# An Lp-pool over 128 MB on one core: three input slots of 51.5 KB per partition in place of four of 32 KB, stores of two loads each, and four smaller loads at the end

## The chip, the cores and the metric

The kernel runs on one core of a Trainium2 chip. Its time is the device time of one execution in microseconds (us). Three of its engines matter here: ACT (ScalarE), DVE (VectorE) and SP (SyncE, which here only sends out transfers). The experiments ran in three sets, each set on one chip beside runs of the kernel before: the control, the quarter rows, the two large end loads and the early half store on one chip, the others on a second. All runs quoted were of the fast state, with a granted clock of 1.000. The profiled executions give a span, from the first to the last instruction; the timed number is about 2 us longer (span 393.7 us, time 395.79 us).

## The reference, cut to what matters

```python
def setup_inputs():
    batch, channels, length = 32, 256, 4096          # 134.2 MB of float32
    ...                                              # p = 2.0, kernel_size = 4

def reference(x, p, kernel_size):
    ...
        window = np.abs(x[:, :, start:end]) ** p
        result[:, :, i] = (np.mean(window, axis=-1)) ** (1.0 / p)
```

Windows do not overlap: four neighbours are squared, summed, divided by four, and the root is taken. So 134.22 MB are read and 33.55 MB written, once each, and any contiguous piece of the flat input whose length is a multiple of four gives a contiguous piece of the output. The kernel is free in how it cuts the data.

## The kernel before

Every load is 128 partitions by 8192 columns (32 KB a row), in four input slots. ACT squares in place, DVE adds groups of four, ACT takes the root in place. Four loads fill one output tile, which is stored at once. All loads go out from SP's queue, most stores from ACT's. The stores of the two groups before the last load are held until all loads have been issued, so that they cover the compute that is left after the last load lands.

```python
    W = 8192
    CH = 4096
    GROUP = 4
    LAST = 1
    ...
    in_pool = ctx.enter_context(tc.tile_pool(name="in_pool", bufs=4))
    out_pool = ctx.enter_context(tc.tile_pool(name="out_pool", bufs=2))
    ...
    def load(i):
        xt = in_pool.tile([P, W], fp32)
        nc.sync.dma_start(out=xt, in_=x_block(i))
    ...
        if i == first + g - 1 and c + CH == W and group_of[i] not in held:
            nc.scalar.dma_start(out=out_block(group_of[i]), in_=ot)
    ...
    for gi in sorted(held):
        nc.sync.dma_start(out=out_block(gi), in_=ots[gi])
```

Of the kernel before, what the change touches and what calls it, by code (L numbers as in the profile page):

```python
# [1 line left out]

# [4 lines left out]


@with_exitstack
def kernel(  # L10
    ctx: ExitStack,
    tc: tile.TileContext,
    x: bass.AP,
    p: float,
    kernel_size: int,
    out: bass.AP,
):








    nc = tc.nc

    assert float(p) == 2.0, "kernel specialized for p == 2"
    k = int(kernel_size)
    assert k == 4, "kernel specialized for kernel_size == 4"  # L30

    P = nc.NUM_PARTITIONS
    fp32 = mybir.dt.float32
    xf = x.rearrange("b c l -> (b c l)")
    of = out.rearrange("b c l -> (b c l)")
    total = xf.shape[0] // P

    W = 8192
    CH = 4096
    GROUP = 4  # L40
    LAST = 1
    n = total // W
    assert n * W == total


    groups = []
    i = 0
    while i < n - LAST:
        g = min(GROUP, n - LAST - i)
        groups.append((i, g))  # L50
        i += g
    groups += [(j, 1) for j in range(n - LAST, n)]
    held = {len(groups) - 1 - LAST - j for j in range(2)}
    group_of = {}
    for gi, (first, g) in enumerate(groups):
        for j in range(g):
            group_of[first + j] = gi

    in_pool = ctx.enter_context(tc.tile_pool(name="in_pool", bufs=4))
    out_pool = ctx.enter_context(tc.tile_pool(name="out_pool", bufs=2))  # L60
    last_pool = ctx.enter_context(tc.tile_pool(name="last_pool", bufs=1))
    ctx.enter_context(tc.manual_schedule())


    def x_block(i):
        first, g = groups[group_of[i]]
        block = xf[first * W * P:(first + g) * W * P].rearrange("(p w) -> p w", p=P)
        return block[:, (i - first) * W:(i - first + 1) * W]

    def out_block(gi):  # L70
        first, g = groups[gi]
        return of[first * W * P // k:(first + g) * W * P // k].rearrange("(p w) -> p w", p=P)

    xts = {}
    ots = {}

    def load(i):
        xt = in_pool.tile([P, W], fp32)
        nc.sync.dma_start(out=xt, in_=x_block(i))  # L79
        xts[i] = xt  # L80

    def root(i, c):
        first, g = groups[group_of[i]]
        ot = ots[group_of[i]]
        at = ((i - first) * W + c) // k
        o = ot[:, at:at + CH // k]
        nc.scalar.activation(  # L87
            out=o, in_=o, func=mybir.ActivationFunctionType.Sqrt, scale=1.0 / k,
        )
        if i == first + g - 1 and c + CH == W and group_of[i] not in held:  # L90
            nc.scalar.dma_start(out=out_block(group_of[i]), in_=ot)

    for i in range(3):
        load(i)

    pending = None
    for i in range(n):
        if i + 3 < n:
            load(i + 3)
        gi = group_of[i]  # L100
        first, g = groups[gi]
        if i == first:
            pool = last_pool if i >= n - LAST else out_pool
            ot = pool.tile([P, g * W // k], fp32)
            ots[gi] = ot
        for c in range(0, W, CH):
            xh = xts[i][:, c:c + CH]
            nc.scalar.activation(  # L108
                out=xh, in_=xh, func=mybir.ActivationFunctionType.Square,
            )  # L110
            at = ((i - first) * W + c) // k
            nc.vector.tensor_reduce(  # L112
                out=ots[gi][:, at:at + CH // k],
                in_=xh.rearrange("p (n j) -> p n j", j=k),
                axis=mybir.AxisListType.X, op=mybir.AluOpType.add,
            )
            if pending is not None:
                root(*pending)
            pending = (i, c)
    root(*pending)  # L120
    for gi in sorted(held):
        nc.sync.dma_start(out=out_block(gi), in_=ots[gi])


# [1 line left out]
_INS = ['x', 'p', 'kernel_size']  # L126
_OUTS = [((32, 256, 1024), 'float32')]

_NUMBERS = {'p': 2.0, 'kernel_size': 4}


# [26 lines left out]
```

## Time and profile before

| | before |
|---|---|
| time, median of the first 3 runs (of 6 with the comparison) | 395.79 us (395.73 us) |
| span | 393.7 us |
| DVE, ACT busy | 282.8 us, 294.7 us |
| bytes moved, mean rate over the span | 167.79 MB, 426 GB/s |
| data packets | 5248, and 656 of 4 B for semaphores (16 for each of the 41 transfers, which signal its end) |

The profile's page of the kernel before. The busy lines give tenths of busy time in 40 equal slices of the span; the DMA line is the mean of the 16 DMA engines, and the line below it what they moved. Then come the packets, the chain of work that ended last by engine, and the costliest groups of instructions (count, busy us, mean ns, idle before and what ended it):

```profile
span 393.7 us, 357 instructions
DVE 282.8 (72%) x64; ACT 294.7 (75%) x130; POOL 0.2 (0%) x4
DMA  8999998999999999999999999999999999999997
GB/s 350 446 430 426 426 426 373 449 446 430 433 426 426 426 430 453 440 430 433 426 426 426 426 449 443 427 433 430 426 426 426 443 446 433 430 433 426 426 435 314
DMA packets 5906, 167.79 MB, mean 426 GB/s; under 512 B 656, under 2 KB 656, under 8 KB 656
DMA 72%; ACT 17%; DVE 9%; SPq 0%; issue 0%; ACTq 0%
...
L112 DVE TENSOR_REDUCE ot<-xt 128x1024 f32<-128x4096 f32 x64 | 282.8, 4420 | 103.4 <-ACT xt L108 102.6
L108 ACT ACTIVATE xt<-xt 128x4096 f32<-128x4096 f32 x64 | 230.9, 3610 | 87.6 <-DMA xt<-in_x_dram 85.0
```

DMA is at nine tenths in every slice but the first, the seventh and the last, while ACT idles a quarter of the time, nearly all of it waiting for loads, and DVE as much, waiting for ACT. The chain is mostly landings of loads. The kernel is bound by the DMA engines, and only what keeps these from moving bytes can cost time.

The waits of SP, which issues the loads, and ACT's wait for the loads (us in total, times, longest us):

```profile
SPq L79 <- DVE ot L112: 293.7, 28, 12.5
SPq L79 <- DMA xt<-in_x_dram: 40.0, 7, 10.2
ACT xt L108 <- DMA xt<-in_x_dram: 85.0, 32, 10.9
```

SP's waits look enormous and cost nothing. SP waits for a slot to come free while the loads already issued are still being moved, as the DMA line shows.

The trace also records each DMA packet with its start, duration and size. In this kernel one row of a transfer is one packet, and for 95% of the time exactly 16 packets are under way, one for each engine. The kept records do not name the engine, so "per engine" below means summed over all packets and divided by 16. These numbers were worked out from those records:

```
size of the row    median duration on one engine
 8,192 B            309 ns
24,576 B            912 ns
32,768 B           1213 ns
first data packet starts at 1.75 us, the last ends at 392.48 us: 390.73 us between them
```

A straight line through these durations has 0.0368 ns per byte (27.2 GB/s on one engine, 435 GB/s on 16) and about 8 ns per packet. The Trainium skill, "DMA: Bandwidth & Descriptors", section "Where 436 GB/s comes from", puts the fabric's ceiling at 435 GB/s, and the slope agrees. The same section says that the HBM side binds at about 358 GB/s for HBM to SBUF; here the measured 426 GB/s decides otherwise. "HBM Reference", section "Specifications (TRN2)", has the reason: the 358 GB/s are a core's share when both cores of a pair stream, and a lone core gets about 425 GB/s, bounded by its DMA engines. No run here had both cores streaming.

### The profile page before, as it was taken

Reading aid. Unit: us, or ns where it says so; the run is one execution under the profiler, and the core shown is the slowest. Engines: PE = TensorE matmul, PEld = TensorE weight load, DVE = VectorE, ACT = ScalarE, POOL = GpSimd, SP = SyncE. Lnnn points to the kernel's source line nnn. Section 1 sums busy time; section 2 is a strip of 40 time slices with the busy share of each in tenths; the row PEclk is TensorE's granted clock in tenths of the full one; section 3 lists DMA queues with packets and bytes.
Section 4 is the critical chain, followed back from the end, with each engine's and each line's share of the span. In section 5 each row is a group of like instructions: output and inputs, shape, how many; then the busy total and the mean of one; then the engine's idle time right before and its main releaser. Section 6 shows DMA issues by size and latency. Waiting matters only on the chain.

```text
span 393.7 us, 357 instructions
## 1 busy us (share of the span) xinstructions
DVE 282.8 (72%) x64; ACT 294.7 (75%) x130; POOL 0.2 (0%) x4
## 2 busy tenths in 40 slices
DVE  0399996739976399764988559866598846999992
ACT  1699987469883798828988189863998819999981
POOL 0000000000000000000000000000000000000000
DMA  8999998999999999999999999999999999999997
GB/s 350 446 430 426 426 426 373 449 446 430 433 426 426 426 430 453 440 430 433 426 426 426 426 449 443 427 433 430 426 426 426 443 446 433 430 433 426 426 435 314
DMA packets 5906, 167.79 MB, mean 426 GB/s; under 512 B 656, under 2 KB 656, under 8 KB 656
## 3 DMA queue, kind: packets, MB, share of 16 engines
q1 hardware_dynamic: 4896, 141.56, 83.9%
q10 hardware_dynamic: 1008, 26.21, 15.5%
q14 instruction: 2, 0.02, 0.0%
HBM read 134.22 MB, written 33.55 MB: 426 GB/s over the span
## 4 chain that ended last, share of the span: by engine, by line
DMA 72%; ACT 17%; DVE 9%; SPq 0%; issue 0%; ACTq 0%
DMA xt<-in_x_dram 72%; ACT xt L108 14%; DVE ot L112 9%; ACT ot L87 2%; SPq L79 0%; ACTq L108 0%
## 5 line engine op out<-in xcount | busy, mean ns | idle before, releaser
L112 DVE TENSOR_REDUCE ot<-xt 128x1024 f32<-128x4096 f32 x64 | 282.8, 4420 | 103.4 <-ACT xt L108 102.6
L108 ACT ACTIVATE xt<-xt 128x4096 f32<-128x4096 f32 x64 | 230.9, 3610 | 87.6 <-DMA xt<-in_x_dram 85.0
L87 ACT ACTIVATE ot<-ot 128x1024 f32<-128x1024 f32 x64 | 67.0, 1047 | 4.2 <-DVE ot L112 3.4
L108 ACT ACT_TABLE_LOAD x1 | 1.3, 1283 | 0.7 <-PEq L139 0.7
L87 ACT ACT_TABLE_LOAD x1 | 1.3, 1283 | 0.0
L139 POOL MEMSET const-uint8-127<- 128x1 uint8 x1 | 0.1, 102 | 0.0
L139 POOL MEMSET const-bfloat16-1.0<- 128x1 bf16 x1 | 0.1, 101 | 0.0
L139 POOL MEMSET const-float32-0.0<- 128x1 f32 x1 | 0.1, 98 | 0.2 <-issue 0.2
L139 POOL MEMSET const-float32-1.0<- 128x1 f32 x1 | 0.1, 98 | 0.0
## 6 DMA issues: line engine op xcount, KB each, us to landing
xt<-in_x_dram SPq DMA_DIRECT2D x32, 4096.0 KB, 35.9
out_dram<-ot ACTq DMA_DIRECT2D x6, 4096.0 KB, 23.2
out_dram<-ot SPq DMA_DIRECT2D x1, 4096.0 KB, 34.1
out_dram<-ot SPq DMA_DIRECT2D x1, 3072.0 KB, 12.3
out_dram<-ot ACTq DMA_DIRECT2D x1, 1024.0 KB, 5.6
```

Of the source, the lines that this page charges most:

```text
L87: nc.scalar.activation(out=o, in_=o, func=mybir.ActivationFunctionType.Sqrt, scale=1.0 / k,)
L108: nc.scalar.activation(out=xh, in_=xh, func=mybir.ActivationFunctionType.Square,)
L112: nc.vector.tensor_reduce(out=ots[gi][:, at:at + CH // k], in_=xh.rearrange("p (n j) -> p n j", j=k), axis=mybir.AxisListType.X, op=mybir. ...
L139: nc = _bacc.Bacc("TRN2", target_bir_lowering=False, num_devices=1)
```

## The change

It uses the memory of a partition differently: three slots of 13,184 columns (51.5 KB) instead of four of 32 KB, and two output tiles of 25.8 KB. There are 18 large loads and four smaller ones, two to a slot, so that the compute left at the end comes in smaller pieces. Two loads make one store, and the last two outputs lie in input slots that are no longer needed. The stores of the last four groups all go out from SP's queue, after all loads. The arithmetic is the same.

```diff
-    W = 8192
-    CH = 4096
-    GROUP = 4
-    LAST = 1
+    W, O_W = 13184, 6592
+    X_SLOTS, O_SLOTS = 3, 2
+    slots = [[(W, [4416, 4384, 4384])]] * 18
+    slots += [[(6592, [3296, 3296])] * 2, [(6592, [3296, 3296]), (5056, [2528, 2528])]]
+    groups = [2] * 9 + [3, 1]
+    late = {7, 8, 9, 10}
+    in_x = {9, 10}
 ... (bookkeeping of loads, groups and columns)
-    in_pool = ctx.enter_context(tc.tile_pool(name="in_pool", bufs=4))
-    out_pool = ctx.enter_context(tc.tile_pool(name="out_pool", bufs=2))
-    last_pool = ctx.enter_context(tc.tile_pool(name="last_pool", bufs=1))
+    x_pool = ctx.enter_context(tc.tile_pool(name="x_pool", bufs=X_SLOTS))
+    o_pool = ctx.enter_context(tc.tile_pool(name="o_pool", bufs=O_SLOTS))
 ...
-    for i in range(3):
-        load(i)
+    while ahead < n and loads[ahead][0] < X_SLOTS - 1:
+        load(ahead)
+        ahead += 1
 ...
-    for gi in sorted(held):
-        nc.sync.dma_start(out=out_block(gi), in_=ots[gi])
+    for g in sorted(late):
+        store(g, nc.sync)
```

More of the change, by code (lines that the diff above doesn't have):

```diff
@@ L33 @@
     fp32 = mybir.dt.float32
+    Act = mybir.ActivationFunctionType
     xf = x.rearrange("b c l -> (b c l)")
@@ L36 @@
     total = xf.shape[0] // P
-    W = 8192
-    CH = 4096
-    GROUP = 4
-    LAST = 1
-    n = total // W
-    assert n * W == total
-    groups = []
-    i = 0
-    while i < n - LAST:
-        g = min(GROUP, n - LAST - i)
-        groups.append((i, g))
-        i += g
-    groups += [(j, 1) for j in range(n - LAST, n)]
-    held = {len(groups) - 1 - LAST - j for j in range(2)}
-    group_of = {}
-    for gi, (first, g) in enumerate(groups):
-        for j in range(g):
-            group_of[first + j] = gi
@@ L59 @@
-    in_pool = ctx.enter_context(tc.tile_pool(name="in_pool", bufs=4))
-    out_pool = ctx.enter_context(tc.tile_pool(name="out_pool", bufs=2))
-    last_pool = ctx.enter_context(tc.tile_pool(name="last_pool", bufs=1))
-    ctx.enter_context(tc.manual_schedule())
-    def x_block(i):
-        first, g = groups[group_of[i]]
-        block = xf[first * W * P:(first + g) * W * P].rearrange("(p w) -> p w", p=P)
-        return block[:, (i - first) * W:(i - first + 1) * W]
-    def out_block(gi):
-        first, g = groups[gi]
-        return of[first * W * P // k:(first + g) * W * P // k].rearrange("(p w) -> p w", p=P)
@@ L74 @@
-    xts = {}
-    ots = {}
-    def load(i):
-        xt = in_pool.tile([P, W], fp32)
-        nc.sync.dma_start(out=xt, in_=x_block(i))
-        xts[i] = xt
-    def root(i, c):
-        first, g = groups[group_of[i]]
-        ot = ots[group_of[i]]
-        at = ((i - first) * W + c) // k
-        o = ot[:, at:at + CH // k]
-        nc.scalar.activation(
-            out=o, in_=o, func=mybir.ActivationFunctionType.Sqrt, scale=1.0 / k,
-        )
-        if i == first + g - 1 and c + CH == W and group_of[i] not in held:
-            nc.scalar.dma_start(out=out_block(group_of[i]), in_=ot)
@@ L93 @@
-    for i in range(3):
-        load(i)
+    W, O_W = 13184, 6592
[5 more added lines that the diff above has]
+    in_x = {9, 10}
+    loads = [(s, sum(w for w, _ in slot[:j]), *slot[j]) for s, slot in enumerate(slots)
+             for j in range(len(slot))]
+    n = len(loads)
+    assert sum(w for _, _, w, _ in loads) == total
@@ new lines, with block @@
+    firsts = [sum(groups[:g]) for g in range(len(groups))]
+    assert sum(groups) == n
+    group_of = [g for g, count in enumerate(groups) for _ in range(count)]
+    columns = [sum(w for _, _, w, _ in loads[firsts[g]:firsts[g] + groups[g]])
+               for g in range(len(groups))]
+    x_pool = ctx.enter_context(tc.tile_pool(name="x_pool", bufs=X_SLOTS))
+    o_pool = ctx.enter_context(tc.tile_pool(name="o_pool", bufs=O_SLOTS))
+    ctx.enter_context(tc.manual_schedule())
+    def block(flat, g, div):
+        at, width = sum(columns[:g]) * P // div, columns[g] * P // div
+        return flat[at:at + width].rearrange("(p w) -> p w", p=P)
@@ new lines, with load, store, root @@
+    slot_tiles = {}
+    xs = {}
+    def load(i):
+        s, at, w, _ = loads[i]
+        if at == 0:
+            slot_tiles[s] = x_pool.tile([P, W], fp32, name="xt")
+        v = slot_tiles[s][:, at:at + w]
+        g = group_of[i]
+        src = sum(loads[j][2] for j in range(firsts[g], i))
+        nc.sync.dma_start(out=v, in_=block(xf, g, 1)[:, src:src + w])
+        xs[i] = v
+    ots = {}
+    def store(g, queue):
+        queue.dma_start(out=block(of, g, k), in_=ots[g])
+    def root(g, o, ends):
+        nc.scalar.activation(out=o, in_=o, func=Act.Sqrt, scale=1.0 / k)
+        if ends and g not in late:
+            store(g, nc.scalar)
@@ L96 @@
+    ahead = 0
+    while ahead < n and loads[ahead][0] < X_SLOTS - 1:
+        load(ahead)
+        ahead += 1
     pending = None
     for i in range(n):
-        if i + 3 < n:
-            load(i + 3)
-        gi = group_of[i]
-        first, g = groups[gi]
-        if i == first:
-            pool = last_pool if i >= n - LAST else out_pool
-            ot = pool.tile([P, g * W // k], fp32)
-            ots[gi] = ot
-        for c in range(0, W, CH):
-            xh = xts[i][:, c:c + CH]
-            nc.scalar.activation(
-                out=xh, in_=xh, func=mybir.ActivationFunctionType.Square,
-            )
-            at = ((i - first) * W + c) // k
+        s, _, w, chunks = loads[i]
+        while ahead < n and loads[ahead][0] < s + X_SLOTS:
+            load(ahead)
+            ahead += 1
+        g = group_of[i]
+        if i == firsts[g]:
+            pool, width = (o_pool, O_W) if g not in in_x else (x_pool, W)
+            t = pool.tile([P, width], fp32, name="ot" if g not in in_x else "xt")
+            ots[g] = t[:, 0:columns[g] // k]
+        at = sum(loads[j][2] for j in range(firsts[g], i)) // k
+        assert sum(chunks) == w
+        c = 0
+        for step in chunks:
+            v = xs[i][:, c:c + step]
+            nc.scalar.activation(out=v, in_=v, func=Act.Square)
+            o = ots[g][:, at + c // k:at + (c + step) // k]
@@ L112 @@
             nc.vector.tensor_reduce(
-                out=ots[gi][:, at:at + CH // k],
-                in_=xh.rearrange("p (n j) -> p n j", j=k),
+                out=o, in_=v.rearrange("p (n j) -> p n j", j=k),
                 axis=mybir.AxisListType.X, op=mybir.AluOpType.add,
@@ L118 @@
                 root(*pending)
-            pending = (i, c)
+            c += step
+            pending = (g, o, i == firsts[g] + groups[g] - 1 and c == w)
     root(*pending)
-    for gi in sorted(held):
-        nc.sync.dma_start(out=out_block(gi), in_=ots[gi])
+    for g in sorted(late):
+        store(g, nc.sync)
 _INS = ['x', 'p', 'kernel_size']
```

## The prediction

> **What bounds the kernel now.** The 16 DMA engines. The page gives 167.79 MB at a mean of 426 GB/s over a span of 393.7 us; the slices show DMA at 9 tenths nearly throughout, while DVE is busy 72% and ACT 75%. The chain of waits that ended last is 72% DMA landing of xt. In the trace's DMA packet records the first data packet starts at 1.8 us and the last ends at 392.5 us; packets follow one another on each engine without gaps. One row is one packet: 32,768 B takes 1213 ns, 24,576 B 912 ns, 8,192 B 309 ns. So a byte costs 0.0368 ns on one engine (27.2 GB/s, 435 GB/s for 16) and a packet about 8 ns more. The Trainium skill, "DMA: Bandwidth & Descriptors", section "Where 436 GB/s comes from", gives 435 GB/s as the fabric's ceiling, which this trace meets; its lower 358 GB/s for one core's HBM share does not bind here.
>
> Beyond that sum (388.6 us per engine) the 390.7 us between first and last packet hold only about 2.1 us: 0.6 us of slow first packets, 1.05 us where all 16 engines' packets took 2.2 us at once (58 us, just after the first store was issued), and about 0.4 us at the end and scattered.
>
> **What the change does.** Bytes are the same. Data packets fall from 5248 to 4224 (22 loads instead of 32, 11 stores instead of 9; 128 each), 64 fewer per engine at about 8 ns: 0.5 us. By size, estimated from the fit: 52,736 B 1947 ns, 26,368 B 978 ns; per engine the sum is 388.0 us against 388.6. Semaphore packets (9 ns each) give under 0.1 us.
>
> Compute moves but is not on the critical path: squares of 4384 columns about 3.85 us, reductions 4.73 us, roots 1.11 us; per load ACT 15.0 us and DVE 14.2 us against 15.6 us of transfer (19.5 with its share of stores). A slot comes free about 18.5 us after landing, when the other two slots still hold about 12 us of queued transfer, so three slots should not starve the queue. The old kernel's waits of loads on DVE (294 us in the waits of the SP queue) cost nothing for the same reason, and stay harmless.
>
> The end: two held stores (7.8 us each) cover the compute left after the last load lands (T, about 368 us). I estimate the store of the three-load group is issued at T+12 and needed at T+15.6, the last one at T+18 and needed at T+21.5; with 1.6 us from issue to data both are in time by some 2 us. The old end was already covered (last small store's data started as the previous store finished, 388.9 us), so nothing is won there beyond a few tenths.
>
> **Predicted:** 395.2 us, range 394.0 to 396.1 (8 in 10). Faster by over 2%: 0.01; within 2%: 0.98; slower by over 2%: 0.01.
>
> **Signs.** Right: DMA still 9 tenths in all middle slices, mean 426 to 428 GB/s, packets 4224 plus 16 per transfer; packets of 52,736 B at 1.94 to 1.96 us; DVE and ACT busy time nearly unchanged (281 and 292 us); no gap in DMA before the last stores; the first load's wait grows from 11 to about 17 us without lengthening the span. Wrong: a slice with DMA at 7 or less before the last one, or SP queue waits after which the rings were empty.
>
> **What would make it wrong.** Rows of 51.5 KB split or slowed; the stall near 58 us vanishing (then about 394.2) or recurring at each store; the late compute slipping by over 2 us, opening a gap before the last two stores; slots freed later than estimated while a store shares the rings.

## The result, and the profile after

The changed kernel took 394.83 us in the median of 6 runs (394.59 to 395.15), the kernel before beside it 395.73 us (395.5 to 395.8). The ratio is 0.9979, with a 95% interval of 0.9966 to 0.9992: a small gain, 0.3 to 1.3 us. A ratio here is the mean time of one kernel's fast runs over that of the other's of the same rounds, so it is not quite the ratio of the medians. As a control in the next set of runs the changed kernel took 394.98 us beside 395.6 us (ratio 0.9983).

The same lines of the changed kernel's page, in the same order:

```profile
span 393.0 us, 316 instructions
DVE 282.4 (72%) x62; ACT 292.4 (74%) x126; POOL 0.2 (0%) x4
DMA  8999999999999999999999999999999999999997
DMA packets 4754, 167.79 MB, mean 427 GB/s; under 512 B 528, under 2 KB 528, under 8 KB 656
DMA 62%; ACT 19%; DVE 14%; issue 2%; ACTq 0%; SPq 0%
...
L110 DVE TENSOR_REDUCE ot<-xt 128x1096 f32<-128x4384 f32 (+1 forms) x54 | 255.4, 4731 | 102.7 <-ACT xt L108 102.4
L108 ACT ACTIVATE xt<-xt 128x4384 f32<-128x4384 f32 (+3 forms) x62 | 230.3, 3716 | 89.2 <-DMA xt<-in_x_dram 86.3
```

There are 1152 fewer packets; the busy times of DVE and ACT are within 1% of before; the DMA line is still full. The chain has less DMA and more compute in it, but with the DMA full throughout that is only another route through the same stretch.

The waits for slots and for the first load (the two views of waits: SP's queue, then the engines; the longest single wait is the last number):

```profile
SPq L75 <- DVE ot L110: 307.7, 17, 18.7
ACT xt L108 <- DMA xt<-in_x_dram: 86.3, 18, 17.5
```

SP's longest wait for a slot grew from 12.5 to 18.7 us, and ACT waits 17.5 us for the first load where it waited 10.9 us. Neither lengthened the span.

From the packet records, for both kernels. "Sum at median" adds each data packet at the median duration of its size, per engine (8,192 B at 309 ns). "Slow" is what packets took over that, per engine. "Idle" is time between the first and the last data packet in which fewer than 16 data packets were under way, counted by how many were missing; most of it (0.86 and 0.82 us) lies at the two ends, where the engines start and finish unevenly. "Overlap" is the same for more than 16, where the records of successive packets overlap:

```
                     before    after
sum at median        388.22   387.74   us per engine
 + slow                2.51     2.11   (first packets 0.61 / 0.65; near 56 to 64 us 1.12 / 0.99; at the end 0.21 / 0)
 + idle                1.01     0.95
 - overlap             1.02     0.82
 = first to last     390.73   389.97
duration of 52,736 B: 1947 ns   of 26,368 B: 978 ns   of 5,056 B: 194 ns
```

Of the 0.75 us between the two traces (by unrounded times), 0.48 us is the packet sum and 0.40 us slow packets, with 0.14 us given back by the rest. The overlap belongs to the packets too: 1.02 us for 328 packets per engine and 0.82 us for 264 are both 3.1 ns per packet. So fewer packets also overlap less, and by these two traces their net gain is 0.28 us. The experiments ask how far that split can be trusted.

### The profile page after: what moved, and what is told of

It reads as the page before. It is cut to its first block, busy times and chain, and to the rows that moved or that the text cites. A ratio compares the mean times of both kernels' runs of the same rounds, so it can differ in the third digit from the quotient of the medians.

```text
span 393.0 us, 316 instructions
## 1 busy us (share of the span) xinstructions
DVE 282.4 (72%) x62; ACT 292.4 (74%) x126; POOL 0.2 (0%) x4
## 4 chain that ended last, share of the span: by engine, by line
DMA 62%; ACT 19%; DVE 14%; issue 2%; ACTq 0%; SPq 0%
DMA xt<-in_x_dram 62%; ACT xt L108 15%; DVE ot L110 11%; DVE xt L110 3%; ACT ot L84 3%; ACT xt L84 1%; ACTq L81 0%; SPq L75 0%; ACTq L108 0%
## 5 line engine op out<-in xcount | busy, mean ns | idle before, releaser
L110 DVE TENSOR_REDUCE ot<-xt 128x1096 f32<-128x4384 f32 (+1 forms) x54 | 255.4, 4731 | 102.7 <-ACT xt L108 102.4
L108 ACT ACTIVATE xt<-xt 128x4384 f32<-128x4384 f32 (+3 forms) x62 | 230.3, 3716 | 89.2 <-DMA xt<-in_x_dram 86.3
L84 ACT ACTIVATE ot<-ot 128x1096 f32<-128x1096 f32 (+1 forms) x54 | 59.8, 1108 | 1.8 <-DVE ot L110 0.9
L110 DVE TENSOR_REDUCE xt<-xt 128x824 f32<-128x3296 f32 (+1 forms) x8 | 27.0, 3384 | 1.3 <-ACT xt L108 1.2
L84 ACT ACTIVATE xt<-xt 128x824 f32<-128x824 f32 (+1 forms) x8 | 6.7, 841 | 3.0 <-DVE xt L110 2.9
```

The source lines that it names most:

```text
L84: nc.scalar.activation(out=o, in_=o, func=Act.Sqrt, scale=1.0 / k)
L108: nc.scalar.activation(out=v, in_=v, func=Act.Square)
L110: nc.vector.tensor_reduce(out=o, in_=v.rearrange("p (n j) -> p n j", j=k), axis=mybir.AxisListType.X, op=mybir.AluOpType.add,)
```

## The experiments

Theory 1: each packet has a cost of its own, and fewer packets are the gain. Theory 2: the gain comes from the new end of the program. Theory 3: it comes from a milder stall at the first store, which both traces show near 57 us.

### Control, and many more packets (theory 1)

> The changed kernel once more, as control for the runs beside it. All theories: 394.8 us, some 0.9 us below the kernel before; packets of 52,736 B at 1947 ns; a stretch near 57 to 61 us in which load packets take 2.2 us or more, as in both first traces.

Measured: 394.98 us (394.74 to 395.05), ratio 0.9983 (0.9971 to 0.9996). Packets of 52,736 B again took 1947 ns, and 1.2 us of slow packets lay between 56 and 64 us.

```diff
-        nc.sync.dma_start(out=v, in_=block(xf, g, 1)[:, src:src + w])
+        cut = 4 if w == W else 1
+        for c in range(0, w, w // cut):
+            nc.sync.dma_start(out=v[:, c:c + w // cut], in_=block(xf, g, 1)[:, src + c:src + c + w // cut])
```

> Each of the 18 large loads goes as four transfers of a quarter row (13,184 B) into the same slot; everything else as in the changed kernel. Theory 1 (the gain is the cost of packets, about 8 ns each): 432 more data packets per engine, 3.3 us, and 54 more semaphore packets of 9 ns, 0.5 us: 398.6 us, above the kernel before; quarter-row packets take about 493 ns. Theory 2 (the gain comes from the new end of the program) and theory 3 (it comes from a milder stall at the first store): the number of packets does not matter, 394.8 us.

Measured: 397.94 us (397.61 to 398.87), ratio 1.0061 (1.0049 to 1.0074). The quarter rows took 493 ns. Its page counts all packets:

```profile
DMA packets 12532, 167.80 MB, mean 424 GB/s; under 512 B 1393, under 2 KB 1393, under 8 KB 1521
```

That is 11,136 data packets and 1392 for semaphores, and 4 others, for the same data. The result is 2.96 us above the control, where 3.8 us was expected: 6.1 ns for each of 486 packets per engine, instead of about 8. The records show why: the packets' own durations grew by 3.59 us, but their overlap grew from 0.81 to 2.17 us, which is again 3.1 ns per packet. A part of a packet's fixed cost runs beside its neighbour. Durations less overlap are 5.2 ns for each of the 432 data packets; most of the rest is idle time at the end, where the engines finish more unevenly (idle is 1.79 us, 1.10 in the control). Theory 1 holds, and for this kernel its size was about a quarter too large; theories 2 and 3 alone are out.

The same in the kernel before, with rows cut in two:

```diff
-        nc.sync.dma_start(out=xt, in_=x_block(i))
+        for c in range(0, W, CH):
+            nc.sync.dma_start(out=xt[:, c:c + CH], in_=x_block(i)[:, c:c + CH])
```

> The kernel before, with each of its 32 loads sent as two transfers of half a row (16,384 B): 256 more data packets and 32 more semaphore packets per engine. Theory 1 (packets cost time, whatever the rest): with the 8 ns of the prediction 2.0 + 0.3 = 2.3 us more; with the slope that the quarter rows showed in the changed kernel (2.96 us for 432 data and 54 semaphore packets, 6.1 ns each of all) 1.75 us more: 397.4 to 398.0 us. Rival (only the form of the end counts): no change.

Measured: 397.71 us (397.51 to 397.78) beside 395.61 us, ratio 1.0051 (1.0039 to 1.0064): 2.10 us for 288 packets per engine, 7.3 ns each. The interval of the ratio alone leaves 5.4 to 8.8 ns, and from first to last packet the trace grew by 2.31 us, 8.0 ns each; so the predicted 8 ns is not excluded here. The change removes 64 data and 8 semaphore packets per engine; at 6.1 to 7.3 ns that is 0.44 to 0.53 us, and the net of its own two traces was 0.28 us. So packets carry a good part of the measured 0.6 to 0.9 us, but not surely all of it. Every kernel here has eight data packets per engine in each transfer, so the times alone do not tell a cost per packet from one per transfer (the 2.96 us of the quarter rows are also 55 ns for each of 54 further transfers). For the change both give the same, for it removes eight transfers; the packets' own durations, which grew, speak for the packets.

### The end of the program (theory 2)

```diff
-    slots += [[(6592, [3296, 3296])] * 2, [(6592, [3296, 3296]), (5056, [2528, 2528])]]
-    groups = [2] * 9 + [3, 1]
+    slots += [[(W, [4416, 4384, 4384])], [(11648, [3904, 3872, 3872])]]
+    groups = [2] * 9 + [1, 1]
```

> The four small loads at the end become two large ones (13,184 and 11,648 columns), each stored alone; the rest as in the changed kernel. Theory 1 alone (packets): the same time, 394.8 us, within 0.2. Theory 2 (the small end loads matter): compute left after the last landing grows to about 19 us, while the held stores cover about 19.5 us less 1.6 us from issue to data, so the queues run dry for 1 to 2 us before the last store: 396 to 397 us, with DMA below 9 tenths in the last but one slice.

Measured: 395.08 us (394.91 to 395.48), ratio 0.9988 (0.9976 to 1.0001). The expected gap is there, but it costs almost nothing. Stretches of 2 us near the end, first the control, then this kernel (us from:to, length, busy time of DVE, ACT and POOL with counts, clock, DMA share, GB/s):

```profile
384.00:386.00 2.00, 2.00 (x1) 0.40 (x1) 0.00 (x0) 1.00 1.06 455
386.00:388.00 2.00, 0.60 (x1) 0.73 (x1) 0.00 (x0) 1.00 0.99 425
388.00:390.00 2.00, 0.00 (x0) 0.00 (x0) 0.00 (x0) 1.00 0.89 376
390.00:392.00 2.00, 0.00 (x0) 0.00 (x0) 0.00 (x0) 1.00 0.52 215
```

```profile
384.00:386.00 2.00, 2.00 (x1) 0.00 (x0) 0.00 (x0) 1.00 1.02 435
386.00:388.00 2.00, 0.34 (x1) 1.01 (x1) 0.00 (x0) 1.00 0.50 211
388.00:390.00 2.00, 0.00 (x0) 0.00 (x0) 0.00 (x0) 1.00 0.89 373
390.00:392.00 2.00, 0.00 (x0) 0.00 (x0) 0.00 (x0) 1.00 0.88 373
```

(A share over 1.00 comes from packets that are counted where they start or end and reach into the next stretch.) With two large end loads the DMA share falls to 0.50 from 386 to 388 us, while DVE and ACT finish the last chunk: the queues are dry. The last store's data starts at 388.24 us, 0.83 us after its issue at 387.41 us. That is half of the 1.6 us that the prediction and this expectation used. Moreover the control loses time in the same place in another way: its share from 390 to 392 us is 0.52, because the 16 engines finish between 391.13 and 391.93 us. In the kernel with the gap the early engines waited in the gap, the last store started nearly level, and all engines finished between 391.74 and 391.90 us. Between the medians lie 0.1 us, which is inside the noise; this kernel also has 16 fewer data packets per engine, worth some 0.1 us at the 6.1 ns found above. So the four small end loads are worth a few tenths of a microsecond at most, and theory 2 in its large form, with 1 to 2 us, falls. By the records the last two stores of the changed kernel follow without a gap: issued at 381.39 and 387.17 us, they were needed at 383.35 and 389.21 us, so with 0.83 us to the first data they were in time by some 1.1 us, not by the 2 us of the prediction.

Is the rest of the gain, what packets do not explain, in how the last store ends? In the kernel before it went out from ACT's queue and had 0.21 us of slow packets.

```diff
-        if i == first + g - 1 and c + CH == W and group_of[i] not in held:
+        if i == first + g - 1 and c + CH == W and group_of[i] not in held | {len(groups) - 1}:
...
-    for gi in sorted(held):
+    for gi in sorted(held | {len(groups) - 1}):
```

> The kernel before, with only its last store (1 MB) moved from ACT's queue to the end of SP's, behind the two held stores, as the changed kernel has it. Theory 2 in its small form (what the packets do not explain, some 0.3 us, comes from the last store, whose 8 KB packets ran between the queues with 0.2 us of slow packets and uneven ends): 395.3 to 395.5 us and no slow packets after 388 us. Rival: no change, 395.7 us; or slower by up to 1 us, if the store's issue from SP comes later.

Measured: 395.46 us (395.23 to 395.62) beside 395.61 us, ratio 0.9996 (0.9983 to 1.001). The slow packets after 388 us are gone, as expected, and from first to last packet it is 390.51 us in place of 390.73 us; but the timed difference lies inside the noise. Nor do these 0.2 us of one trace belong to the end alone: the end gave 0.21 us and a smaller stall near 58 us another 0.2 us, while 0.26 us more idle time took as much back. So it is inconclusive.

### The stall at the first store (theory 3)

In both kernels some load packets near 57 us take far longer than their kind: 16 packets of 2.1 to 2.4 us before (1.21 us is normal), as many as there are engines, and 29 of 2.1 to 3.1 us after (1.95 us is normal). In the windows of 4 us, first the kernel before, then the changed one:

```profile
52.00:56.00 4.00, 3.09 (x2) 4.00 (x2) 0.00 (x0) 1.00 1.19 516
56.00:60.00 4.00, 3.85 (x1) 3.55 (x2) 0.00 (x0) 1.00 0.89 270
```

```profile
52.00:56.00 4.00, 2.81 (x2) 3.58 (x2) 0.00 (x0) 1.00 0.98 422
56.00:60.00 4.00, 3.44 (x2) 3.96 (x2) 0.00 (x0) 1.00 0.96 336
```

The DMA share stays near 0.9, for the engines are busy, but the rate falls to 270 and 336 GB/s. Busy does not mean moving at full speed. The first store was issued at 56.38 and 55.62 us, and its first packets moved at 61.66 and 59.62 us; the slow packets are loads, mostly between the two. To see whether the store brings it, its first half was sent 16 us earlier:

```diff
+    early = [False, False, False, True, False, False]
 ...
+        if g == 0 and early.pop():
+            nc.scalar.dma_start(out=block(of, 0, k)[:, :W // k], in_=ots[0][:, :W // k])
```

(The list `early` lets this through once, after the root of the first load's last chunk. The second half follows where the whole store stood.)

> The first store is cut in two, and its first half goes out as soon as the first load is worked (about 37 us in place of 56 us), same queue. Theory 3 (the 1 us stall near 57 us belongs to the first store): the slow load packets move to 38 to 43 us and none stays near 57 to 61 us; time within 0.3 us of 394.8, as the stall is only moved. Rival (the stall belongs to that time of the execution or to the loads): it stays near 57 us.

Measured: 394.98 us (394.73 to 395.86), ratio 0.9988 (0.9975 to 1.0002). The half store was issued at 39.88 us; 0.97 us of slow packets lie between 40 and 52 us and none near 57 us, where the second half passed without any. The stall belongs to the first store and keeps its size of about 1 us. (The quarter rows say the same: there the first store was issued at 47.62 us, and the stall, 0.71 us, lies near 50 us.) As the source of the gain theory 3 falls: the stall is 1.12 us in the trace of before and 0.93 us in that of the kernel before with its last store moved, and 0.99 and 1.21 us in the two traces of the changed kernel.

Two kernels then asked which first use it is, by a tiny store of 128 rows of 32 B of zeros, which the true results overwrite later. Both gave correct results.

```diff
+    first = ctx.enter_context(tc.tile_pool(name="first", bufs=1)).tile([P, 8], fp32, name="first")
+    nc.vector.memset(first, 0.0)
+    nc.scalar.dma_start(out=block(of, 0, k)[:, 0:8], in_=first)
     ahead = 0
```

> The changed kernel with one tiny store (128 rows of 32 B of zeros into the first output block, later overwritten by the true results) issued by ACT at the very start, beside the first loads. Theory A (the 1 us of slow load packets belongs to the first use of the store path, ACT's queue or writes to HBM): no slow packets near 57 to 61 us any more; they come in the first microseconds, where they partly hide behind the 0.6 us of slow first packets: 394.0 to 394.8 us. Rival (it belongs to the first large store): still about 1 us of slow packets near 57 to 61 us, time 394.9 us.

Measured: 394.69 us (394.55 to 394.91), ratio 0.9976 (0.9964 to 0.9989); 0.72 us of slow packets near 56 to 62 us.

```diff
+    nc.sync.dma_start(out=block(of, 0, k)[:, 0:8], in_=first)
     pending = None
```

(with the same tile and memset, after the first two loads)

> The same tiny store, but issued by SP in the loads' queue after the first two loads. If the stall belongs to the first write to HBM by any queue: none near 57 to 61 us. If it belongs to the first use of ACT's queue: still about 1 us near 57 to 61 us, as in the changed kernel. Time 394.6 to 395.2 us either way; the place of the slow packets decides.

Measured: 394.77 us (394.6 to 395.0), ratio 0.9979 (0.9965 to 0.9993); 1.05 us of slow packets there.

So neither the first use of ACT's queue nor the first write to HBM takes the stall away: it comes with the first large store. The 0.3 us by which it is smaller after the tiny store from ACT, and the time of 394.69 us, are inside what single traces and times differ by. The intervals of these kernels and of the changed one overlap, so no version here is shown to beat it.

### Three slots, and what a dry queue costs

The prediction said that three slots keep about 12 us of loads queued and that two would leave none.

```diff
-    X_SLOTS, O_SLOTS = 3, 2
+    X_SLOTS, O_SLOTS = 2, 4
-    in_x = {9, 10}
+    in_x = set()
```

> Two input slots in place of three (and four output slots, so that the last two outputs need no input slot). The prediction's theory (a slot comes free about 18.5 us after its load landed, against 15.6 us of transfer; three slots leave some 12 us of queued transfer, two leave none): the loads' queue runs dry some 3 to 5 us per load, the stores fill a part of it: 400 to 430 us, with DMA at 8 tenths or less in many middle slices. Rival (slots do not matter, the DMA is kept full by the stores): 395 us.

Measured: 434.76 us (434.13 to 435.2), ratio 1.0988, above the 400 to 430 us expected. Its page's DMA line, and SP's waits for slots:

```profile
DMA  9994999979997999799979997999989989798998
...
SPq L75 <- DVE ot L110: 326.4, 18, 18.8
```

About every fourth slice (a slice is 10.8 us) falls to 7 or 8, so the queue runs dry about once in every pair of loads. SP's longest wait is 18.8 us, as with three slots (18.7 us); there it was free, and here it stops the stream. Yet the engines' idle time between first and last packet is only 27.7 us, against 40 us lost. The rest is slow packets: 15.9 us per engine, against 2.1 us in the changed kernel. They come at each restart of the loads (0.6 to 0.7 us) and, again, at each of the seven stores from ACT's queue (0.7 to 1.4 us within 9 us of its issue). The first of the held stores, which goes out from SP's queue, has 1.0 us just before its first data. In the kernels with three slots the first store paid this and the later ones 0.05 us or less. That suggested a rule: a large store pays when it is the first after the loads' stream has started anew. One forced dry spell tests it, by a load that must wait for a tiny memset on DVE:

```diff
-        while ahead < n and loads[ahead][0] < s + X_SLOTS:
+        while ahead < n and loads[ahead][0] < s + X_SLOTS - (i == 9):
...
+        if i == 11:
+            nc.vector.memset(v[:, 0:8], 0.0)
```

> The changed kernel with one forced dry spell of the loads' queue: the load into slot 12 of 20 waits until the work on the load two before it is done, by a tiny memset that VectorE reaches only then. Theory (a store costs about 1 us of slow load packets only when it is the first after the loads' queue has started anew, as the seven stores of the two-slot kernel suggest): a gap of 3 to 5 us near 200 us, slow packets of 0.7 us at the restart, and about 0.7 to 1 us of slow packets again at the one next store, none at those after it. Rival (only the first store of an execution costs it): slow packets at the restart, none at the next store. Time 398 to 401 us either way.

Measured: 398.25 us (398.09 and 398.41), ratio 1.0065 (1.0047 to 1.0084). The windows around it:

```profile
200.00:204.00 4.00, 3.79 (x2) 2.47 (x2) 0.00 (x0) 1.00 1.00 435
204.00:208.00 4.00, 2.23 (x2) 0.72 (x1) 0.00 (x0) 1.00 1.04 382
208.00:212.00 4.00, 0.80 (x1) 4.00 (x2) 0.00 (x0) 1.00 0.80 343
212.00:216.00 4.00, 3.95 (x1) 3.58 (x2) 0.00 (x0) 1.00 1.03 369
216.00:220.00 4.00, 3.52 (x1) 4.00 (x3) 0.00 (x0) 1.00 0.93 343
220.00:224.00 4.00, 3.96 (x2) 2.33 (x2) 0.00 (x0) 1.00 0.94 409
```

The control, in the windows of the store that follows:

```profile
212.00:216.00 4.00, 3.89 (x1) 3.58 (x2) 0.00 (x0) 1.00 0.97 422
216.00:220.00 4.00, 3.59 (x1) 4.00 (x3) 0.00 (x0) 1.00 1.17 508
```

In the kernel with the dry spell the load was issued at 206.31 us. By the records the engines finish the load before it between 205.9 and 206.9 us and start again at 207.3 us: 1.16 us of idle on average, less than the 3 to 5 us expected, because the store issued at 173 us had shared the engines until 198.7 us and so delayed that load. Then come 0.64 us of slow packets at the restart, and 1.25 us of slow packets at the next store, issued at 212.20 us: the rate is 369 and 343 GB/s from 212 to 220 us at a full DMA share. The stores at 254 and 293 us have 0.00 and 0.03 us. In the control, as in every kernel that kept its loads going, the same store had none, with two loads under way or queued as here, so the length of the queue does not explain it. So the rule held, here (one trace) and in the stores of the two-slot kernel that suggested it, and the rival (only the first store of an execution pays) is out. Idle 1.16, restart 0.64 and store 1.25 us add up to 3.05 of about 3.3 us over the control of the first set. Why the first store after a start slows the loads is not shown by any run.

## Why the prediction was right

Point by point, in the prediction's own order:

- **"What bounds the kernel now: the 16 DMA engines."** Right. The DMA line is full before and after, and DVE's and ACT's busy times, which the prediction put at 281 and 292 us, were 282.4 and 292.4 us without any trace of them in the time.
- **Packets "at about 8 ns".** The mechanism was right: durations of 1947 and 978 ns were measured as estimated, and the counts came out as 4224 data packets. The term was probably somewhat too large. Two kernels with more packets gave 6.1 and 7.3 ns for each; 8 ns stays possible for the second. The prediction counted durations alone and left out that each packet's record overlaps the next by 3.1 ns, whatever its length. For the change the slopes make 0.44 to 0.53 us, and the net of its own traces 0.28 us, where the prediction had 0.5 us and under 0.1 us for semaphores.
- **"Three slots should not starve the queue."** Right, and the margin was wider than the 12 us stated, which left out the stores' share of the engines: when SP issued a load at 148.05 us, the two loads before it landed only at 148.8 and 168.2 us (ACT starts on them there), so some 20 us of transfer, with a store's share, were still queued. The prediction's own 19.5 us per load with that share would have given 2 x 19.5 - 18.5 = 20.5 us. With two slots the queue ran dry and 40 us were lost.
- **The end, "in time by some 2 us".** In time, yes; the margin was about 1.1 us. The last load landed at 368.7 us (368 predicted); the last two stores were issued at T+12.7 and T+18.5 (12 and 18 predicted) and needed at T+14.6 and T+20.5 (15.6 and 21.5 predicted). The 1.6 us from issue to data, read from a store that had to wait for the engines, was 0.83 us where the queue was empty.
- **The stall near 58 us.** It did not vanish and did not recur at later stores, which the prediction had as its two ways to fail. It took 1.12 us before and 0.99 to 1.21 us after.
- **The time.** 395.2 us was predicted and 394.83 us measured, inside the range of 394.0 to 396.1 us. That range also holds the 395.73 us of the kernel before, so the number alone would have come out right with no gain at all; what tests the mechanism are the packet durations and the two kernels with more packets. The predicted gain was 0.6 us, the measured ones 0.9 and 0.6 us in two sets of runs. What packets do not explain, 0.1 to 0.6 us, may be scatter of the runs (the interval of the gain is 0.3 to 1.3 us) or the slow packets at the end of the kernel before (0.21 us); the run that took those away gained 0.15 us with an interval that includes zero, so this part stays open.

## What to carry to other kernels

When the DMA line is full from first slice to last, larger transfers could win little more here than the cost of the packets they save (6 to 8 ns per packet and engine): count the packets before rebuilding the buffers. Then check the one thing that a new buffer plan can lose, whether the load queue still has work when a slot comes free; a queue that runs dry costs more than its idle time, because the packets after the restart and those around the next store are slow as well. A gap before the last store need not cost its full length either, when the engines would finish unevenly without it.

## What the Trainium skill lacked or had wrong

- "DMA: Bandwidth & Descriptors", section "Why small descriptors are slow (HBM only)", speaks of a fixed overhead of about 3 cycles per packet, with a descriptor of 256 B as its example. It has no time measured with long rows: here, with rows of 13 to 52 KB on 16 engines, a further packet cost 6.1 to 7.3 ns of the kernel's time (semaphore packets counted alike), and the fit gives about 8 ns in its own duration, of which 3.1 ns ran beside the next packet.
- The same page, section "Where 436 GB/s comes from", says that the HBM side (about 358 GB/s) binds for HBM to SBUF. For one core alone the runs show 426 and 427 GB/s over the whole span. The sentence lacks the condition that both cores of a pair stream; the page's own measured table and "HBM Reference" have it.
- No page that I read says that the first large store after the loads' stream has started slows the load packets by a total of 0.7 to 1.4 us per engine, and again after each restart, while the stores in an unbroken stream cost 0.05 us or less. Its cause is open.
- "DMA: Bandwidth & Descriptors", section "Latency and other measured facts", gives about 0.6 us as the first-byte latency of transfers issued from SP and ACT, and does not say from when it counts. Here it was 0.83 us for a store on an empty queue, 0.95 us for a load after a dry spell and 1.0 us for the first load, from the start of the issuing instruction to the first data packet; from the end of that instruction (0.33 to 0.38 us long) it was 0.50, 0.62 and 0.63 us, which agrees. That the first packets after a restart are together slow by another 0.6 to 0.7 us per engine stands on no page that I read.
